# Weight sums of a seven-product matmul formed by accumulating DMAs instead of VectorE additions

## The chip, the cores and the metric

The kernel runs on one core of a Trainium2 chip. Its metric is the device time of one execution in microseconds, the median of several runs. The profiler records one execution on that core. Engines in the profile: PE (TensorE matmul) and PEld (its weight loads), DVE (VectorE), ACT (ScalarE), POOL (GpSimd), SP (SyncE, which here only issues DMAs).

## The reference

One layer of a hybrid decoder over 256 prompt tokens and 8 decoding sequences of one token, 264 columns in all. A half-step SwiGLU, a mixing block (mLSTM heads beside a short gated convolution), a second half-step SwiGLU, a last RMSNorm. What the change touches is the first half of both SwiGLUs:

```python
D_MODEL, D_FF = 2048, 5504
def swiglu(x, wg, wu, wd):
    return (jax.nn.silu(x @ wg) * (x @ wu)) @ wd
...
h = h + 0.5 * swiglu(rmsnorm(h, norm_ffn1[l]), ffn1_gate[l], ffn1_up[l], ffn1_down[l])
```

## The kernel before, in words

All weights come from HBM as f32 in blocks of 128 x 128. Each is multiplied in three f16 products: ACT writes the f16 high part (`high`), DVE the f16 remainder (`low`), and PE takes high x high, high x low, low x high. A SwiGLU has 43 column blocks j of gate (g) and up (u). An ordinary block is two `product` calls, g and u, of 16 k blocks each, made in two halves of 8 k blocks: 24 matmuls a half. Before each half stands a `fetch`: SP loads 512 KB of weights that are used five halves later (`wraw`, six buffers), ACT writes `whi`, DVE writes `wlo`.

For 11 of the 43 blocks in the first SwiGLU and 12 in the second (`SEVEN`), gate and up together are made by Strassen's scheme in Winograd's form: seven products of half size instead of eight. The weight's four quarters are g and u, each with an upper and a lower half of the k blocks; the tokens are split in a left and a right half of 132, whose sums are the `forms`. `chunk_by_seven` makes the products in two chunks: chunk 0 (72 matmuls of 132 columns) with three quarters as they are, from the tiles `sa0` (high) and `sa1` (low); chunk 1 (96 matmuls) with four sums of quarters, from `sb0` and `sb1`. The order of the blocks from a seven-block j on is: chunk 0 of j, the ordinary block j + 1 (four halves), chunk 1 of j, the ordinary block j + 2 (four halves), chunk 0 of the next seven-block. One such block is a period of the program.

The tiles for the chunks are prepared in small steps between the halves: after each half's matmuls and its fetch, `prepare_step` takes the next step of a table (`prepare`). There are 8 steps per seven-block, and the table says at which step of its block a function runs: POOL issues four loads of 512 KB (`load`, tile `sraw`, at steps -2 and -1), ACT and DVE cut the three quarters into `sa0` and `sa1` (`blocks`, `blocks_low`, steps 2 to 4), DVE forms the four sums in `ssum` by three additions or subtractions per half (`all_sums`), and ACT and DVE cut these into `sb0` and `sb1` (steps 5 to 8). Chunk 0 follows step 7, chunk 1 follows step 11, which is step 3 of the next block. All of a block's data is loaded in the block before, into two buffers. The first block of a layer runs its steps three earlier. The steps stop during most of the down products between the 22nd and 23rd column block.

Nothing reorders the instructions: each engine runs its queue in the order in which the code issues it and waits on semaphores. `Norm.form` builds the sums of token halves on POOL; `by_seven` adds the seven products up on DVE; `activated` multiplies silu(g) by u and cuts the result for the down product. A check of sums decides at the end whether a second, slower pass is run.

Of the kernel before, what the change touches and what calls it, by code (L numbers as in the profile page):

```python
# [8 lines left out]
F32 = mybir.dt.float32  # L9
# [3 lines left out]
ALU = mybir.AluOpType  # L13
# [38 lines left out]
TH = T // 2  # L52
# [93 lines left out]
def step(ctx: ExitStack, tc: tile.TileContext, a: dict, shared, bad=None):  # L146
    nc = tc.nc
# [70 lines left out]
    def high(dst, src, scale=1.0):  # L218

        if half_size or not isinstance(scale, float):  # L220
            nc.scalar.activation(dst, src, AF.Copy, scale=scale)  # L221
        else:
            nc.scalar.copy(dst, src)
# [49 lines left out]
    def at(delta, fn, *args):  # L273
        agenda.setdefault(int(seq[0]) + delta, []).append((fn, args))
# [43 lines left out]
    def prepare(pool, layer):  # L318

        gu = a[f"w{layer}gu"]
        ks = [slice(0, 4), slice(4, 8)]
        raws = [None, None]
        steps.clear()
        step_no[0] = None

        def load(j, c):
            raws[c] = raw = pool.tile([128, 4, 4, 128], F32, tag="raw", name="sraw", bufs=2)
            for g in range(2):  # L330
                blocks = gu[j, g].rearrange("p (s k) m -> p s k m", s=2)
                queue.dma_start(raw[:, 2 * g : 2 * g + 2], blocks[:, :, ks[c], :])  # L332

        def blocks(j, c):
            if c == 0:
                formed[j, 0] = [
                    pool.tile([128, 3, 8, 128], PART, tag=f"sa{i}", name=f"sa{i}")
                    for i in range(2)
                ]
            high(formed[j, 0][0][:, :, ks[c]], raws[c][:, 0:3], sw)  # L340

        def blocks_low(j, c):
            hi, lo = formed[j, 0]
            low(lo[:, :, ks[c]], raws[c][:, 0:3], hi[:, :, ks[c]], sw)

        sums = [None]

        def all_sums(j, c):
            raw = raws[c]
            if c == 0:  # L350
                formed[j, 1] = [
                    pool.tile([128, 4, 8, 128], PART, tag=f"sb{i}", name=f"sb{i}")
                    for i in range(2)
                ]
            sums[0] = s = pool.tile([128, 4, 4, 128], F32, tag="ssum", name="ssum")
            nc.vector.tensor_tensor(s[:, 2], raw[:, 2], raw[:, 3], op=ALU.add)
            nc.vector.tensor_tensor(s[:, 3], s[:, 2], raw[:, 1], op=ALU.subtract)
            nc.vector.tensor_tensor(  # L358
                s[:, 0:2], raw[:, 0:4:2],
                s[:, 3].unsqueeze(1).to_broadcast([128, 2, 4, 128]), op=ALU.subtract,  # L360
            )
            high(formed[j, 1][0][:, :, ks[c]], s, sw)

        def sums_low(j, c):
            hi, lo = formed[j, 1]
            low(lo[:, :, ks[c]], sums[0], hi[:, :, ks[c]], sw)

        for n, j in enumerate(SEVEN[layer]):
            for s, fn, c in (
                (2, blocks, 0), (3, blocks_low, 0), (3, blocks, 1), (4, blocks_low, 1),  # L370
                (5, all_sums, 0), (6, sums_low, 0), (7, all_sums, 1), (8, sums_low, 1),
            ):
                steps.setdefault(8 * n + s - (3 if n == 0 else 0), []).append((fn, j, c))
            for c in range(2):
                s = -4 if n == 0 else 8 * n + (-2, -1)[c]
                steps.setdefault(s, []).append((load, j, c))

    def prepare_step():
        if step_no[0] is not None and step_no[0] < step_end[0]:
            for fn, j, c in steps.get(step_no[0], ()):  # L380
                fn(j, c)
            step_no[0] += 1

    def chunk_by_seven(j, c, x, forms, banks):
# [242 lines left out]
    class Norm:  # L627
# [26 lines left out]
        def form(self, k):  # L654


            b = tmp.tile([128, 7, TH], F32, tag="y7", name="form_b", bufs=1)
            t = tmp.tile([128, 4, TH], F32, tag="form_t", name="form_t", bufs=2)
            for i, kb in enumerate((k + 8, k)):
                nc.scalar.activation(  # L660
                    b[:, 2 * i : 2 * i + 2].rearrange("p s t -> p (s t)"), h[kb], AF.Copy,
                    scale=gains[:, self.col + kb : self.col + kb + 1],
                )
            side.tensor_tensor(t[:, 0:2], b[:, 1:4:2], b[:, 0:2], op=ALU.subtract)
            side.tensor_tensor(t[:, 2], b[:, 3], t[:, 0], op=ALU.subtract)
            side.tensor_tensor(t[:, 3], t[:, 2], b[:, 2], op=ALU.subtract)
            self.parts = t

        def form_split(self, k):
# [56 lines left out]
    def ffn(layer, norm, done, start=None, end=None):  # L726
        with ExitStack() as stack:
# [10 lines left out]
            first = True  # L738
            seven = {}

            def activated(j, i, zu, sg):
                nc.vector.tensor_tensor(zu, zu, sg, op=ALU.mult)
                act[j] = t = apool.tile([128, 2, T], PART, tag=f"a{i}", name=f"a{i}")
                high(t[:, 0, :], zu, sa[layer])
                rest = t[:, 1, :], zu, t[:, 0, :], sa[layer]
                if lag[0] and j < blocks[-1] - 2:
                    at(1.5, low, *rest)
                else:
                    low(*rest)

            def by_seven(j, i):


                p, q, r = (b[:, : 3 * TH].rearrange("p (n t) -> p n t", n=3) for b in seven[j])
# [24 lines left out]
                at(1, halves)  # L779
                at(2, activated, j, i, z[:, 1], sg)  # L780

            if half_size:
                spool = stack.enter_context(tc.tile_pool(name=f"seven_{norm.tag}", bufs=1))
# [896 lines left out]
```

## Time and profile before

| | |
|---|---|
| median of 3 runs | 1814.26 us (1813.57 to 1816.54) |
| span of the profiled execution, first to last instruction | 1812.0 us |
| PE busy | 1796.6 us |
| DVE, ACT, POOL busy | 1391.5, 958.0, 250.2 us |
| HBM read | 366.72 MB |
| POOL's loads of sraw | 92 of 512 KB |

The profiled execution's own device time is not among the figures; its span stands in for it, 2.3 us below the median. A row of the profile reads: line, engine, operation, tile written <- tiles read, shape, count | busy time in all, mean ns of one | idle time of the engine just before, and what ended it. PE's matmuls overlap, so that a row's mean is longer than the distance from one to the next.

### The profile page before, as it was taken

To read this page: it belongs to the slowest core of one execution; us is meant where nothing else is said; L and a number is where in the kernel's file an instruction comes from. 1 tells how busy PE (TensorE), PEld (TensorE's weight loads), DVE (VectorE), ACT (ScalarE), POOL (GpSimd) and SP (SyncE) were. 2 spreads that over 40 slices of the span, in tenths; PEclk is the share of its full clock that TensorE was granted. 3 is DMA by queue.
4 is the path that set the end of the run, shared out by engine and by line. 5 is a ranking of instruction groups with operands and counts; after the bars stand their busy time and mean duration, and the time that the engine had idled before them with its cause. 6 is when DMAs were issued, how large, how long until landed. Compare 5 with 4: busy or idle time off the path is not lost.

```text
span 1812.0 us, 42493 instructions
## 1 busy us (share of the span) xinstructions
PE 1796.6 (99%) x17920; PEld 1590.5 (88%) x17920; DVE 1391.5 (77%) x2132; ACT 958.0 (53%) x1329; POOL 250.2 (14%) x339
## 2 busy tenths in 40 slices
PE   9999999999999999999999999999999999999997
PEld 7889988899998888888888888889988889999886
DVE  7888985579997667788888766789986459998554
ACT  7664554445554444667566645655554435554442
POOL 0310000000100222222121022410000001010131
PEclk9999999999999999999999999999999999999999
DMA  9765666645654565988887655756567646564663
GB/s 300 251 219 170 218 225 212 202 157 191 217 189 151 187 190 193 307 279 273 282 282 241 221 179 185 253 191 221 190 187 257 199 147 213 193 209 155 190 193 97
DMA packets 118503, 381.34 MB, mean 210 GB/s; under 512 B 14972, under 2 KB 24796, under 8 KB 118304
## 3 DMA queue, kind: packets, MB, share of 16 engines
q1 hardware_dynamic: 95856, 302.29, 51.1%
q0 software_dynamic: 21504, 75.81, 12.4%
q8 instruction: 142, 2.33, 0.5%
q10 hardware_dynamic: 944, 0.45, 0.1%
q14 instruction: 57, 0.47, 0.1%
HBM read 366.72 MB, written 11.78 MB: 209 GB/s over the span
## 4 chain that ended last, share of the span: by engine, by line
PE 98%; DVE 1%; DMA 0%; ACT 0%; issue 0%; SPq 0%; DVEq 0%; ACTq 0%
PE ps L288 28%; PE ps L290 28%; PE ps L289 28%; PE ps L410 12%; PE ps L506 1%; PE ps L624 0%; PE ps L1349 0%; PE ps L1292 0%; PE ps L1247 0%; DMA wraw<-in_w1gu 0%; DVE sq L698 0%; DVE h L918 0%; PE ps L1270 0%; PE ps L1333 0%; PE ps L1271 0%; ACT whi L221 0%
## 5 line engine op out<-in xcount | busy, mean ns | idle before, releaser
L229 DVE SCALAR_TENSOR_TENSOR wlo<-wraw,whi 128x1024 f16<-128x1024 f32 (+2 forms) x600 | 695.2, 1181 | 97.3 <-ACT whi L221 96.9
L221 ACT ACTIVATE whi<-wraw 128x1024 f16<-128x1024 f32 (+2 forms) x600 | 585.0, 1001 | 202.3 <-PE ps L289 166.8
L290 PE MATMUL ps<-x,wlo 128*128 128x264 f16 x1952 | 539.4, 276 | 0.0
L288 PE MATMUL ps<-x,whi 128*128 128x264 f16 x1952 | 539.4, 276 | 0.0
L289 PE MATMUL ps<-x,whi 128*128 128x264 f16 x1952 | 539.4, 276 | 0.0
L289 PEld LDWEIGHTS <-whi 128*128 128x128 f16 x4522 | 442.2, 98 | 66.4
L288 PEld LDWEIGHTS <-whi 128*128 128x128 f16 x4522 | 442.5, 98 | 65.3 <-issue 0.6
L290 PEld LDWEIGHTS <-wlo 128*128 128x128 f16 x4522 | 442.3, 98 | 65.2
L288 PE MATMUL ps<-a,whi 128*128 128x264 f16 (+2 forms) x1418 | 383.3, 273 | 0.0
L289 PE MATMUL ps<-a,whi 128*128 128x264 f16 (+2 forms) x1418 | 383.3, 273 | 0.0
L290 PE MATMUL ps<-a,wlo 128*128 128x264 f16 (+2 forms) x1418 | 383.2, 273 | 0.0
L288 PE MATMUL ps<-xm,whi 128*128 128x264 f16 x896 | 247.6, 276 | 0.0
L289 PE MATMUL ps<-xm,whi 128*128 128x264 f16 x896 | 247.6, 276 | 0.0
L290 PE MATMUL ps<-xm,wlo 128*128 128x264 f16 x896 | 247.6, 276 | 0.0
L221 ACT ACTIVATE sb<-ssum 128x2048 f16<-128x2048 f32 x46 | 87.9, 1910 | 177.3 <-DVE ssum L358 177.3
L410 PEld LDWEIGHTS <-sb 128*128 128x128 f16 x2208 | 128.8, 98 | 0.7
L860 DVE SCALAR_TENSOR_TENSOR h<-ps,h 128x264 f32<-128x264 f32 x62 | 26.8, 432 | 130.5 <-PE ps L290 130.5
L229 DVE SCALAR_TENSOR_TENSOR sb<-ssum,sb 128x2048 f16<-128x2048 f32 x46 | 105.3, 2289 | 6.0 <-ACT sb L221 3.6
L410 PE MATMUL ps<-f,sb 128*128 128x132 f16 x1656 | 99.0, 221 | 0.0
L410 PEld LDWEIGHTS <-sa 128*128 128x128 f16 x1656 | 97.1, 98 | 0.7
L332 POOL DMA_DIRECT2D sraw<-in_w2gu x48 | 34.6, 722 | 420.3 <-issue 382.0
L332 POOL DMA_DIRECT2D sraw<-in_w1gu x44 | 31.7, 723 | 392.5 <-issue 359.3
(256 smaller groups left out, 1665.9 us busy)
## 6 DMA issues: line engine op xcount, KB each, us to landing
wraw<-in_w2gu SPq DMA_DIRECT2D x124, 512.0 KB, 4.6
wraw<-in_w1gu SPq DMA_DIRECT2D x120, 512.0 KB, 4.9
wraw<-in_win SPq DMA_DIRECT2D x112, 512.0 KB, 5.6
wraw<-in_w1d SPq DMA_DIRECT2D x80, 448.0 KB, 4.1
wraw<-in_w2d SPq DMA_DIRECT2D x80, 448.0 KB, 3.8
sraw<-in_w2gu POOLq DMA_DIRECT2D x48, 512.0 KB, 5.3
sraw<-in_w1gu POOLq DMA_DIRECT2D x44, 512.0 KB, 5.3
wraw<-in_wout SPq DMA_DIRECT2D x32, 512.0 KB, 4.8
```

Source lines behind the costliest of these rows:

```text
L221: nc.scalar.activation(dst, src, AF.Copy, scale=scale)
L229: nc.vector.scalar_tensor_tensor(dst, src, scale, hi, op0=ALU.mult, op1=ALU.subtract)
L288: nc.tensor.matmul(ps, wh, xk[:, 0, :], start=first, stop=False)
L289: nc.tensor.matmul(ps, wh, xk[:, 1, :], start=False, stop=False)
L290: nc.tensor.matmul(ps, wl, xk[:, 0, :], start=False, stop=last)
L332: queue.dma_start(raw[:, 2 * g : 2 * g + 2], blocks[:, :, ks[c], :])
L410: nc.tensor.matmul(out, w[:, f, k, :], b(k)[:, part, :], start=(k + term == 0), stop=(k == 7 and term == 2),)
L506: nc.tensor.matmul(ps[j0 + j], w[:, nk * j + k, :], x[k0 + k][:, part, :], start=(k0 + k + n == 0), stop=(k0 + k == KB - 1 and n == 2),)
L860: nc.vector.scalar_tensor_tensor(h[db], ps, 0.5 / (sw * sa[layer]), h[db], op0=ALU.mult, op1=ALU.add)
```

## The change

The signs of the scheme are turned so that the four sums of weight quarters are all plain sums: lower g + lower u; upper u + lower u; that plus lower g; that plus upper g. `sraw` now holds three quarters of a block (lower and upper as loaded by `upper` and `lower`), from which `sa` is cut. Then POOL issues DMAs with `accum_op=add` (`adds`), which add another quarter from HBM to what lies in the tile: one into two slots at once, two more into one slot. After each of them the slots concerned are cut into `sb` (`cut` for the high part on ACT, `cut_rest` for the remainder on DVE). DVE's three additions and `ssum` are gone. Since `sraw` is overwritten, an add must wait for the cuts before it, and a cut for the add before it. The turned signs cost one subtraction more per form on POOL and a negative scale in `activated`.

```diff
-        def load(j, c):
...
-            sums[0] = s = pool.tile([128, 4, 4, 128], F32, tag="ssum", name="ssum")
-            nc.vector.tensor_tensor(s[:, 2], raw[:, 2], raw[:, 3], op=ALU.add)
-            nc.vector.tensor_tensor(s[:, 3], s[:, 2], raw[:, 1], op=ALU.subtract)
-            nc.vector.tensor_tensor(
-                s[:, 0:2], raw[:, 0:4:2],
-                s[:, 3].unsqueeze(1).to_broadcast([128, 2, 4, 128]), op=ALU.subtract,
-            )
-            high(formed[j, 1][0][:, :, ks[c]], s, sw)
...
+        def upper(j):
+            raws[j] = raw = pool.tile([128, 3, 8, 128], F32, tag="raw", name="sraw", bufs=2)
+            queue.dma_start(raw[:, 2], gu[j, 1][:, 0:8, :])
+            queue.dma_start(raw[:, 1], gu[j, 0][:, 8:16, :])
+
+        def lower(j):
+            queue.dma_start(raws[j][:, 0], gu[j, 0][:, 0:8, :])
+
+        def adds(j, slots, g, s):
+            dst, src = raws[j][:, slots], gu[j, g][:, 8 * s : 8 * s + 8, :]
+            n = slots.stop - slots.start
+            if n > 1:
+                src = src.unsqueeze(1).to_broadcast([128, n, 8, 128])
+            queue.dma_start(dst, src, accum_op=ALU.add)
...
+        def cut(j, c, slots, of):
+            hi, lo = tiles(j, c)
+            high(hi[:, slots], raws[j][:, of], sw)
+
+        def cut_rest(j, c, slots, of):
+            hi, lo = tiles(j, c)
+            low(lo[:, slots], raws[j][:, of], hi[:, slots], sw)
+
+        one, two, three_ = slice(0, 1), slice(1, 3), slice(2, 3)
         for n, j in enumerate(SEVEN[layer]):
-            for s, fn, c in (
-                (2, blocks, 0), (3, blocks_low, 0), (3, blocks, 1), (4, blocks_low, 1),
-                (5, all_sums, 0), (6, sums_low, 0), (7, all_sums, 1), (8, sums_low, 1),
+            for s, fn, *what in (
+                (2, cut, 0, two, two), (3, cut_rest, 0, two, two), (3, adds, two, 1, 1),
+                (3, cut, 0, one, one), (4, cut_rest, 0, one, one),
+                (6, cut, 1, two, two), (7, cut_rest, 1, two, two), (7, adds, three_, 0, 1),
+                (9, cut, 1, slice(3, 4), three_), (9, cut_rest, 1, slice(3, 4), three_),
+                (9, adds, three_, 0, 0),
+                (11, cut, 1, one, three_), (11, cut_rest, 1, one, three_),
             ):
...
+            side.tensor_tensor(b[:, 4], b[:, 1], b[:, 0], op=ALU.subtract)
+            side.tensor_tensor(t[:, 2], b[:, 4], b[:, 3], op=ALU.subtract)
+            side.tensor_tensor(t[:, 3], t[:, 2], b[:, 2], op=ALU.add)
...
-                high(t[:, 0, :], zu, sa[layer])
-                rest = t[:, 1, :], zu, t[:, 0, :], sa[layer]
+                high(t[:, 0, :], zu, sign * sa[layer])
+                rest = t[:, 1, :], zu, t[:, 0, :], sign * sa[layer]
```

How this moves instructions is shown for the second seven-block of the first layer (j = 13) and its neighbours. The numbers behind the names tell buffers apart; the brackets name the semaphores that an instruction waits for (DMASW: one of POOL's DMAs).

POOL's queue before, over one block: the four loads of the next block, and the first of the one after.

```order
L332 DMA sraw_2237<-in_w1gu 128x2x512 [waits DMASW5_49,DMASW6_49,DVE_49,Activation_49]
L332 DMA sraw_2237<-in_w1gu 128x2x512
L332 DMA sraw_2275<-in_w1gu 128x2x512 [waits DMASW0_49,DMASW7_49,DVE_49,Activation_49]
L332 DMA sraw_2275<-in_w1gu 128x2x512
L332 DMA sraw_2717<-in_w1gu 128x2x512 [waits DMASW1_49,DMASW2_49,DVE_49,Activation_49]
```

And after: `sraw_1765` is the block's own tile, `sraw_2234` the next block's. L329, L330 and L333 are loads, L340 the adds.

```order
L340 DMA sraw_1765<-in_w1gu 128x2x1024 [waits DMASW7_49,DMASW0_49,DVE_49]
L329 DMA sraw_2234<-in_w1gu 128x1024 [waits DMASW6_49,DMASW3_49]
L330 DMA sraw_2234<-in_w1gu 128x1024
L340 DMA sraw_1765<-in_w1gu 128x1024 [waits DMASW2_49,DVE_49]
L333 DMA sraw_2234<-in_w1gu 128x1024
L340 DMA sraw_1765<-in_w1gu 128x1024 [waits DMASW5_49,DVE_49]
L340 DMA sraw_2234<-in_w1gu 128x2x1024 [waits DMASW3_49,DMASW4_49,DVE_49,Activation_49]
```

Three adds of the block now stand between the loads for the next one, each waiting for DVE (the remainder cut before it) and for a DMA.

ACT before, from step 6 to the cuts of step 11 (`sb0_2190` is the block's, `sa0_2459` the next block's; `a` and `tb` belong to ordinary blocks or to by_seven):

```order
L221 ACTIVATE whi_2232<-wraw_2230 128x1024 [waits DMAHW6_49,PE_49]
L221 ACTIVATE whi_2266<-wraw_2264 128x1024 [waits DMAHW7_49,PE_49]
L221 ACTIVATE sb0_2190<-ssum_2270 128x4x512 [waits DVE_49]
L221 ACTIVATE a12_2281<-tc_2278 128x264 [waits DVE_49]
L221 ACTIVATE whi_2388<-wraw_2386 128x1024 [waits DMAHW0_49,PE_49,Activation_49]
L221 ACTIVATE whi_2419<-wraw_2417 128x1024 [waits DMAHW1_49,PE_49,Activation_49]
L808 ACTIVATE tb_2426<-ta_2423 128x264 [waits DVE_49,Activation_49]
L221 ACTIVATE whi_2455<-wraw_2453 128x1024 [waits DMAHW2_49,PE_49,Activation_49]
L221 ACTIVATE sa0_2459<-sraw_2237 128x3x512 [waits DMASW2_49,DMASW1_49]
L221 ACTIVATE whi_2488<-wraw_2486 128x1024 [waits DMAHW3_49,PE_49,Activation_49]
L221 ACTIVATE sa0_2459<-sraw_2275 128x3x512 [waits DMASW4_49,DMASW3_49]
```

And after, the same stretch:

```order
L221 ACTIVATE whi_2227<-wraw_2225 128x1024 [waits DMAHW6_49,PE_49]
L221 ACTIVATE sb0_2231<-sraw_1765 128x2048 [waits DMASW2_49]
L221 ACTIVATE whi_2263<-wraw_2261 128x1024 [waits DMAHW7_49,PE_49]
L221 ACTIVATE a12_2273<-tc_2270 128x264 [waits DVE_49]
L221 ACTIVATE whi_2380<-wraw_2378 128x1024 [waits DMAHW0_49,PE_49,Activation_49]
L221 ACTIVATE whi_2410<-wraw_2408 128x1024 [waits DMAHW1_49,PE_49,Activation_49]
L221 ACTIVATE sb0_2231<-sraw_1765 128x1024 [waits DMASW5_49]
L806 ACTIVATE tb_2420<-ta_2417 128x264 [waits DVE_49,Activation_49]
L221 ACTIVATE whi_2449<-wraw_2447 128x1024 [waits DMAHW2_49,PE_49,Activation_49]
L221 ACTIVATE sa0_2453<-sraw_2234 128x2048 [waits DMASW4_49,DMASW3_49]
L221 ACTIVATE whi_2482<-wraw_2480 128x1024 [waits DMAHW3_49,PE_49,Activation_49]
L221 ACTIVATE sb0_2231<-sraw_1765 128x1024 [waits DMASW7_49]
```

The cuts of `sb0` no longer wait for DVE but for POOL's DMAs, and the last of them, formerly three steps before chunk 1, stands behind the last whi of step 11.

PE at the border from step 11 to chunk 1, after:

```order
L290 MATMUL ps_2422<-x115_484,wlo_2228 128x264
L405 LDWEIGHTS sb0_2231 [waits Activation_49]
L405 MATMUL ps_2277<-x10_189,sb0_2231 128x132
L405 LDWEIGHTS sb0_2231
L405 MATMUL ps_2277<-x10_189,sb0_2231 128x132
L405 LDWEIGHTS sb1_2232 [waits DVE_49]
L405 MATMUL ps_2277<-x10_189,sb1_2232 128x132
```

The first matmul of chunk 1 reads the slot that is cut last, and waits there for ACT, then for DVE; before, the same rows had no wait.

More of the change, by code (lines that the diff above doesn't have):

```diff
@@ L322, in prepare @@
         gu = a[f"w{layer}gu"]
-        ks = [slice(0, 4), slice(4, 8)]
-        raws = [None, None]
+        raws, parts = {}, {}
         steps.clear()
         step_no[0] = None
-        def load(j, c):
[L329 to L337, printed above, removed]
+        def upper(j):
+            raws[j] = raw = pool.tile([128, 3, 8, 128], F32, tag="raw", name="sraw", bufs=2)
+            queue.dma_start(raw[:, 2], gu[j, 1][:, 0:8, :])
+            queue.dma_start(raw[:, 1], gu[j, 0][:, 8:16, :])
@@ new lines, in lower, with tiles @@
+        def lower(j):
[6 more added lines that the diff above has]
+            queue.dma_start(dst, src, accum_op=ALU.add)
+        def tiles(j, c):
+            if (j, c) not in formed:
+                formed[j, c] = [
+                    pool.tile([128, 3 + c, 8, 128], PART, tag=f"s{'ab'[c]}{i}", name=f"s{'ab'[c]}{i}")
@@ L338, in blocks @@
                     for i in range(2)
                 ]
[L340 to L354, printed above, removed]
-            sums[0] = s = pool.tile([128, 4, 4, 128], F32, tag="ssum", name="ssum")
-            nc.vector.tensor_tensor(s[:, 2], raw[:, 2], raw[:, 3], op=ALU.add)
-            nc.vector.tensor_tensor(s[:, 3], s[:, 2], raw[:, 1], op=ALU.subtract)
-            nc.vector.tensor_tensor(
-                s[:, 0:2], raw[:, 0:4:2],
-                s[:, 3].unsqueeze(1).to_broadcast([128, 2, 4, 128]), op=ALU.subtract,
-            )
-            high(formed[j, 1][0][:, :, ks[c]], s, sw)
@@ L364, in sums_low @@
-        def sums_low(j, c):
-            hi, lo = formed[j, 1]
-            low(lo[:, :, ks[c]], sums[0], hi[:, :, ks[c]], sw)
-        for n, j in enumerate(SEVEN[layer]):
-            for s, fn, c in (
-                (2, blocks, 0), (3, blocks_low, 0), (3, blocks, 1), (4, blocks_low, 1),
-                (5, all_sums, 0), (6, sums_low, 0), (7, all_sums, 1), (8, sums_low, 1),
-            ):
[L373 to L376, printed above, removed]
+            return formed[j, c]
@@ new lines, in cut @@
+        def cut(j, c, slots, of):
[5 more added lines that the diff above has]
+        one, two, three_ = slice(0, 1), slice(1, 3), slice(2, 3)
+        for n, j in enumerate(SEVEN[layer]):
+            for s, fn, *what in (
[5 more added lines that the diff above has]
+                (11, cut, 1, one, three_), (11, cut_rest, 1, one, three_),
+            ):
+                steps.setdefault(8 * n + s - (3 if n == 0 else 0), []).append((fn, j, *what))
+            for fn, s in ((upper, -2), (lower, -1)):
+                s = -4 if n == 0 else 8 * n + s
+                steps.setdefault(s, []).append((fn, j))
@@ L378, in prepare_step @@
     def prepare_step():
         if step_no[0] is not None and step_no[0] < step_end[0]:
-            for fn, j, c in steps.get(step_no[0], ()):
-                fn(j, c)
+            for fn, *what in steps.get(step_no[0], ()):
+                fn(*what)
             step_no[0] += 1
@@ L663, in form @@
                 )
-            side.tensor_tensor(t[:, 0:2], b[:, 1:4:2], b[:, 0:2], op=ALU.subtract)
-            side.tensor_tensor(t[:, 2], b[:, 3], t[:, 0], op=ALU.subtract)
-            side.tensor_tensor(t[:, 3], t[:, 2], b[:, 2], op=ALU.subtract)
+            side.tensor_tensor(
+                t[:, 0:2], b[:, 0:4:3], b[:, 1:2].to_broadcast([128, 2, TH]), op=ALU.subtract
+            )
+            side.tensor_tensor(b[:, 4], b[:, 1], b[:, 0], op=ALU.subtract)
+            side.tensor_tensor(t[:, 2], b[:, 4], b[:, 3], op=ALU.subtract)
+            side.tensor_tensor(t[:, 3], t[:, 2], b[:, 2], op=ALU.add)
             self.parts = t
@@ L739, in ffn, with activated @@
             seven = {}
-            def activated(j, i, zu, sg):
+            def activated(j, i, zu, sg, sign=1.0):
                 nc.vector.tensor_tensor(zu, zu, sg, op=ALU.mult)
                 act[j] = t = apool.tile([128, 2, T], PART, tag=f"a{i}", name=f"a{i}")
-                high(t[:, 0, :], zu, sa[layer])
-                rest = t[:, 1, :], zu, t[:, 0, :], sa[layer]
+                high(t[:, 0, :], zu, sign * sa[layer])
+                rest = t[:, 1, :], zu, t[:, 0, :], sign * sa[layer]
                 if lag[0] and j < blocks[-1] - 2:
@@ L779, in by_seven @@
                 at(1, halves)
-                at(2, activated, j, i, z[:, 1], sg)
+                at(2, activated, j, i, z[:, 1], sg, -1.0)
             if half_size:
```

## Prediction

> **What bounds the kernel now.** I read the page's engine totals first, then the chain, then what PE waited for. The columns are busy time and its share of the span; in the chain, shares of the span.
>
> ```profile
> span 1812.0 us, 42493 instructions
> PE 1796.6 (99%) x17920; PEld 1590.5 (88%) x17920; DVE 1391.5 (77%) x2132; ACT 958.0 (53%) x1329; POOL 250.2 (14%) x339
> PE 98%; DVE 1%; DMA 0%; ACT 0%; issue 0%; SPq 0%; DVEq 0%; ACTq 0%
> ...
> PE ps L975 <- DVE ok L969: 2.3, 1, 2.3
> PE ps L506 <- ACT whi L221: 1.8, 2, 1.3
> PE ps L624 <- DVE sq L700: 1.2, 1, 1.2
> ```
>
> PE is the chain, and its three longest waits, all at the two ends of the program, make 5.3 us. No wait on sa, sb or a form is among them. DVE work that goes away can therefore give back nothing that shows; the question is only whether PE starts to wait. So I went to one block made by seven (layer 1, j = 13): its row in a view by stretches (PE busy, ..., clock, DMA share, GB/s), its chunks in the chain, and PE's rows at their borders.
>
> ```profile
> 147.00:178.26 31.26, 31.26 (x362) 28.44 (x361) 28.56 (x39) 16.56 (x20) 2.88 (x4) 1.00 0.61 202
> ...
> 116.83 4.14 PE ps L410 x72
> 148.09 4.14 PE ps L410 x72
> 163.03 5.52 PE ps L410 x96
> ...
> 147.92 0.57 PE L410 MATMUL ps<-x,sa 128*128 128x132 f16 x7
> 154.65 0.28 PE L290 MATMUL ps<-x,wlo 128*128 128x264 f16 x1
> 154.76 0.28 PE L288 MATMUL ps<-x,whi 128*128 128x264 f16 x1
> 162.86 0.85 PE L410 MATMUL ps<-x,sb 128*128 128x132 f16 x12
> ```
>
> A block takes 31.26 us, all of it PE, at clock 1.00, with the DMA engines busy 61%. There are 11 + 12 = 23 such blocks. The chunk on sa (4.14 us) is issued from 147.92, the chunk on sb from 162.86, and a half product of 24 matmuls takes (162.86 - 147.92 - 4.14) / 4 = 2.70 us. I count the block's steps as the table does: step 7 is the last half before the sa chunk, step 11 the last before the sb chunk. 154.76 is the start of step 9.
>
> **What is removed.** Three DVE adds per half block, and the cuts of their sums:
>
> ```profile
> L358 DVE TENSOR_TENSOR ssum<-sraw,ssum 128x1024 f32<-128x1024 f32 x46 | 56.3, 1225 | 1.6
> L357 DVE TENSOR_TENSOR ssum<-ssum,sraw 128x512 f32<-128x512 f32 x46 | 31.8, 692 | 1.6
> L356 DVE TENSOR_TENSOR ssum<-sraw 128x512 f32<-128x512 f32 x46 | 31.5, 686 | 0.0
> L229 DVE SCALAR_TENSOR_TENSOR sb<-ssum,sb 128x2048 f16<-128x2048 f32 x46 | 105.3, 2289 | 6.0 <-ACT sb L221 3.6
> L221 ACT ACTIVATE sb<-ssum 128x2048 f16<-128x2048 f32 x46 | 87.9, 1910 | 177.3 <-DVE ssum L358 177.3
> L229 DVE SCALAR_TENSOR_TENSOR wlo<-wraw,whi 128x1024 f16<-128x1024 f32 x420 | 509.5, 1229 | 51.9 <-ACT whi L221 51.7
> L221 ACT ACTIVATE whi<-wraw 128x1024 f16<-128x1024 f32 x420 | 425.9, 1044 | 100.5 <-PE ps L289 89.5 <-PE ps L1271 2.6 <-DVE wlo L229 1.9
> ```
>
> 56.3 + 31.8 + 31.5 = 119.6 us of DVE go, 5.2 us per block, all beside PE: worth 0. The seven tiles are cut either way, in five pieces now instead of four (two of 128x2048 and three of 128x1024): on ACT 2 x 1.91 + 3 x 1.04 = 6.9 us per block, on DVE 2 x 2.29 + 3 x 1.23 = 8.3 us. ACT, busy 16.56 of 31.26, and DVE, 28.56 less 5.2, cover that. The negated scale and the turned signs change constants in the same instructions: 0.
>
> **What is added on POOL.** One subtraction more per form, 16 in all. POOL's rows around the last form of layer 1 and its loads:
>
> ```profile
> 103.16 0.96 POOL L666 TENSOR_TENSOR form_t<-form_t,form_b 128x132 f32<-128x132 f32 x1
> 147.11 1.44 POOL L332 DMA_DIRECT2D sraw<-in_w1gu  x2 [28.70 <-issue]
> ```
>
> At 0.96 us each that is 15 us of an engine that is 14% busy; the last form ends at 104.1, the first chunk that reads forms starts at 116.83, so 12.7 us cover it, also with the first accumulating transfer queued ahead of that form. Worth 0. A block issues six DMAs instead of four, at 0.72 us each: 4.3 us of 31.26, no bound either.
>
> **What becomes a chain.** Before, everything needed for sb lay in SBUF when DVE turned to it. Now it comes through three transfers in a row, each held back by the cut of the tile that it changes: cut two slots, add (two slots), cut two, add (one slot), cut, add (one slot), cut; and the sb chunk reads the slot cut last first. I call the landing times of the last two adds D. Where the chain starts is read from DVE and ACT before:
>
> ```profile
> 143.89 0.69 DVE L356 TENSOR_TENSOR ssum<-sraw 128x512 f32<-128x512 f32 x1
> 146.48 0.43 DVE L805 TENSOR_TENSOR ta<-ps,rstd 128x264 f32<-128x264 f32 x1
> 146.90 0.42 DVE L742 TENSOR_TENSOR y<-y,tb 128x264 f32<-128x264 f32 x1
> 148.41 0.41 ACT L808 ACTIVATE tb<-ta 128x264 f32<-128x264 f32 x1
> 148.72 0.41 ACT L221 ACTIVATE a<-y 128x264 f16<-128x264 f32 x1
> 149.04 1.99 ACT L221 ACTIVATE whi<-wraw 128x1024 f16<-128x1024 f32 x2
> ```
>
> Without the adds ta starts at 143.9 instead of 146.5. ACT then goes tb at 144.3, a 0.31 later, whi another 0.32 later (the spacings of the rows), and after 0.95 us of whi the cut of step 6 at 145.9. It ends at 145.9 + 1.91 = 147.8, the rest on DVE at 147.8 + 2.29 = 150.1: issue of the second add. It lands at 150.1 + D; cut 1.04, rest 1.23: the third add goes out at 152.4 + D, lands at 152.4 + 2D, and its cut ends at 153.4 + 2D. PE wants that tile at 162.86, so it is late by 2D - 9.4; and the rest, 1.23 us later, is wanted two matmuls (0.1 us) after the tile: another 1.1. PE waits **2D - 8.3 us per block**.
>
> There is a floor that doesn't depend on the second add. The cut of step 9 stands on ACT behind that step's whi, whose buffer PE frees with the last matmul of step 8 (154.65 + 0.28 = 154.9; that ACT waits for PE there is the 89.5 us in whi's row). It starts no earlier than 154.9 + 0.95 = 155.9, the third add goes out at 155.9 + 1.04 + 1.23 = 158.2, and the last cut ends at 159.2 + D. PE waits at least **D - 2.55 us per block**; this rules from D = 5.8 down.
>
> Behind the waiting cut stand, on ACT, the next block's single-slot cut of sa, a of the neighbouring product and m of the sb chunk; on DVE the next block's rests; on POOL its first add. None of them has a reader that PE reaches before the sb chunk, and the weights of the four halves after it are cut before the wait. So the wait itself is all that PE sees.
>
> **The price D.** No transfer of this trace accumulates. The nearest rows, landing times from issue (sraw over the whole run; sraw around this block; rb and SP's weights, as listed by issue; the POOL queue's packets, MB and share of the engines):
>
> ```profile
> DMA to landing us min/median/max: 4.3/5.3/12.3
> DMA to landing us min/median/max: 4.7/5.1/6.7
> rb<-dr POOLq DMA_DIRECT2D x16, 512.0 KB, 8.3
> ...
> wraw<-in_w1gu SPq DMA_DIRECT2D x120, 512.0 KB, 4.9
> q0 software_dynamic: 21504, 75.81, 12.4%
> ```
>
> An add of 512 KB must bring the old 512 KB as well as the new: as many bytes read as a pair of plain loads. The pair's second goes out 0.72 us after the first and lands at most 6.7 later here: D = 7.4. The lower end is a plain load: 4.3 at least, 5.1 as a rule. Above stand rb with 8.3 and the longest sraw, 12.3. I take 7.4, the row with the same bytes to read. Then PE waits 2 x 7.4 - 8.3 = 6.5 us per block, 23 x 6.5 = 150 us, and the span is 1812.0 + 150 = 1962. The median of the runs, 1814.26, lies 2.3 above the profiled span, which I add: **1964 us**. I keep 23 alike: the first block of a layer starts three steps earlier, the one at j = 22 has two of its adds done during the down products, and the second of a layer follows a block that started early; these go both ways.
>
> The first add (two slots) is no bound at this price. By q0's row a pass of 512 KB takes 0.124 x 1812 x 0.524 / 75.81 = 1.55 us of all engines; two passes more than a one-slot add make 7.4 + 3.1 = 10.5. It goes out when both rests that follow the stalled chunk's start are done, 1.1 + 2.29 = 3.4 us after that start, and is wanted at step 6: the sb chunk's 5.52 and its wait of 1.1, four halves of 2.70, less the 2.0 from 145.9 to 147.92, are 15.4 after it. It has 12.0 us.
>
> [...]
>
> **Rivals.**
> 1. The adds land like plain loads, D = 4.3 to 5.8. Then the floor rules: at 5.1, 2.55 x 23 = 59 us, 1873 us (1854 at 4.3). For it: engines idle 39% of a block; the adds go out alone. Against: the bytes.
> 2. Dearer adds, D over 9. At 10 the wait is 11.7 us a block, 2083 us; at the longest row, 12.3, 16.3 and 2189, where the transfers themselves come near to the pace. 0.61 x 31.26 = 19.1 us of engine time now move the twelve transfers of 512 KB of a block, 6.3 MB; the new block loads 5.8 MB plainly and writes 2.1 MB by adds, at twice the time per byte 30 us, at four times 43 us, more than a block has. For it: one wait adds to the next, and SP's weights share the engines. Against: SP's loads land in 4.9 us beside POOL's today, rb's in 8.3.
> 3. Not slower: the whole chain is hidden, and PE keeps its 1796.6 us. The place is the last add, the point D <= 2.55 from the floor. The time would be 1814, no less, since there is no PE wait to recover. Against: no sraw load, none of them an add, landed in under 4.3.
>
> A wrong sum would send the program into its second pass and roughly double the time; the signs work out on paper, and I give that nothing of its own.
>
> **How the numbers follow.** Forecast (D from 5.8 to 9, 1890 to 2037): 0.55. Rival 1: 0.20. Rival 2: 0.20. Rival 3: 0.05, of which 0.02 for a gain from something I don't see. The range leaves about one in ten on each side: low 1866, between D = 4.3 and 5.1 of rival 1; high 2090, D = 10. A measurement of this kernel can tell about 0.2% (3.6 us) from no change: faster 0.02, same 0.03, slower 0.95.
>
> **What would show it.** In the new trace PE's waits have one large entry, on sb from the cuts and their rests, some 23 times each and nowhere else; the sb chunks lie 31.3 + 6.5 us apart; the sa chunk still follows without a gap; clock 1.00; the three ssum lines are gone and DVE is busy about 120 us less. A landing time of about 7.4 for the one-slot adds shows D, about 10 or 11 for the first. What would make it wrong: D far from 7.4 either way, each us of it being 46 us of time; ACT reaching the cut of step 6 later than 145.9, each us 23; or waits of PE on whi, which would mean that ACT, held by its waits for the adds, no longer keeps the plain weights ahead.

## The result, and the profile after

The changed kernel takes 1963.85 us in the median (1958.47 to 1971.83), the kernel before 1813.91 us beside it: a ratio of 1.083, interval 1.080 to 1.086. The profiled execution took 1971.83 us, with a span of 1970.1, so 158.1 us more than the profiled span before; it was the longest of the four executions. The prediction said 1964. As will be seen, two of its errors cancelled.

From the page of the kernel after: span, PE's and DVE's busy time, POOL's DMA queue (packets, MB, share of the engines' time), the chain by engine. Then what PE waited for (us in all, times, longest), and the landing times of all accumulating transfers.

```profile
span 1970.1 us, 42493 instructions
PE 1847.4 (94%) x17920; PEld 1630.0 (83%) x17920; DVE 1282.2 (65%) x2017; ACT 968.2 (49%) x1352; POOL 300.4 (15%) x401
q0 software_dynamic: 31072, 111.99, 23.9%
PE 51%; DMA 17%; issue 16%; DVE 10%; ACT 5%; POOL 0%; DVEq 0%; ACTq 0%; POOLq 0%; SPq 0%
```

```profile
PE ps L405 <- ACT sb L221: 87.8, 22, 8.0
PE ps L405 <- DVE sb L229: 20.9, 23, 1.0
```

```profile
DMA to landing us min/median/max: 5.4/6.7/10.7
```

PE was 98% of the chain and is now 51%; DMA, ACT and DVE, which did not count, share the rest. Two waits have appeared, both at the head of the sb chunk and nowhere else: 87.8 + 20.9 = 108.7 us. That leaves 158.1 - 108.7 = 49.4 us without a wait. They are in PE's own busy time: 1847.4 against 1796.6, for the same 17920 matmuls. Where they come from shows in a view by stretches (PE busy with its count, ..., granted clock, DMA share, GB/s): one whole block first, then the stretch of the wait and the two that follow it.

```profile
446.31:483.31 37.00, 33.20 (x361) 29.95 (x361) 23.76 (x34) 16.98 (x20) 4.66 (x6) 0.95 0.79 214
...
478.50:483.31 4.81, 1.01 (x10) 0.51 (x7) 1.28 (x2) 2.36 (x3) 0.00 (x0) 1.00 0.79 266
483.31:487.00 3.69, 3.69 (x38) 3.69 (x39) 3.25 (x5) 0.42 (x1) 0.99 (x2) 0.57 0.00 0
487.00:490.35 3.35, 3.35 (x59) 3.35 (x57) 0.18 (x1) 0.00 (x0) 1.38 (x3) 0.96 0.63 95
```

A block took 31.26 us before and takes 37.00 here. Of the 5.74 us more, 37.00 - 33.20 = 3.80 are PE standing still (one of the shorter waits; the mean is 108.7 / 23 = 4.7), and 33.20 - 31.26 = 1.94 are PE working for longer on the same instructions. The last two rows say why: right after the wait the granted clock is 0.57 for about 3.7 us, then it is back at 0.96. That is (1 - 0.57) x 3.69 + (1 - 0.96) x 3.35 = 1.6 + 0.1 = 1.7 us of full clock less. In the same 3.69 us the DMA engines moved nothing at all (share 0.00), so that traffic can't be what holds PE there.

The chain of this block, in order of time (start, us, what; L405 is the sb chunk), shows the wait's origin:

```profile
461.80 1.81 ACT sb L221
...
463.63 2.30 DVE sb L229
465.93 0.29 issue
466.22 5.38 DMA sraw<-in_w1gu
...
471.65 2.95 issue
...
474.61 6.31 DMA sraw<-in_w1gu
...
480.94 1.06 ACT sb L221
...
482.03 1.24 DVE sb L229
...
483.31 7.22 PE ps L405 x94
```

What ACT and DVE did in the 2.95 us after the second add had landed:

```profile
471.05 1.06 ACT L221 ACTIVATE whi<-wraw 128x1024 f16<-128x1024 f32 x1 [2.91 <-PE ps L289]
472.01 1.04 ACT L221 ACTIVATE sb<-sraw 128x1024 f16<-128x1024 f32 x1
...
473.08 1.23 DVE L229 SCALAR_TENSOR_TENSOR sb<-sraw,sb 128x1024 f16<-128x1024 f32 x1 [3.16 <-ACT sb L221]
```

These are the links that the prediction strung together: the cut of two slots, its rest, the second add (5.38 us to land), the third (6.31), the last cut and rest. The 2.95 us between the two adds are mostly work: the second add lands at 466.22 + 5.38 = 471.60, its cut starts 0.4 us later, behind the whi of step 9 on ACT, and the cut and its rest take 2.3 us. The chunk that follows takes 7.22 us for 94 matmuls; before, all 96 took 5.52.

### The profile page after: what moved, and what is told of

The parts are those of the page before. It is cut to its first block, busy times and chain, and to the rows that moved or that the text cites. A ratio compares the mean times of both kernels' runs of the same rounds, so it can differ in the third digit from the quotient of the medians.

```text
span 1970.1 us, 42493 instructions
## 1 busy us (share of the span) xinstructions
PE 1847.4 (94%) x17920; PEld 1630.0 (83%) x17920; DVE 1282.2 (65%) x2017; ACT 968.2 (49%) x1352; POOL 300.4 (15%) x401
## 3 DMA queue, kind: packets, MB, share of 16 engines
q0 software_dynamic: 31072, 111.99, 23.9%
## 4 chain that ended last, share of the span: by engine, by line
PE 51%; DMA 17%; issue 16%; DVE 10%; ACT 5%; POOL 0%; DVEq 0%; ACTq 0%; POOLq 0%; SPq 0%
PE ps L288 13%; PE ps L290 13%; PE ps L289 13%; DMA sraw<-in_w2gu 9%; DMA sraw<-in_w1gu 8%; PE ps L405 8%; DVE sb L229 4%; ACT sb L221 3%; DVE wlo L229 2%; DVE sa L229 1%; ACT whi L221 1%; PE ps L501 1%; DMA wraw<-in_w1gu 1%; DVE ta L803 0%; PE ps L619 0%
## 5 line engine op out<-in xcount | busy, mean ns | idle before, releaser
L405 PEld LDWEIGHTS <-sb 128*128 128x128 f16 x2208 | 167.0, 116 | 120.2 <-ACT sb L221 94.1
L229 DVE SCALAR_TENSOR_TENSOR sb<-sraw,sb 128x1024 f16<-128x1024 f32 (+1 forms) x69 | 109.1, 1581 | 225.9 <-ACT sb L221 225.9
L405 PE MATMUL ps<-x,sb 128*128 128x132 f16 x552 | 62.9, 296 | 108.8 <-ACT sb L221 87.8
L221 ACT ACTIVATE sb<-sraw 128x1024 f16<-128x1024 f32 (+1 forms) x69 | 92.1, 1335 | 95.0 <-DMA sraw<-in_w2gu 51.9
L405 PE MATMUL ps<-f,sb 128*128 128x132 f16 x1656 | 117.8, 241 | 0.0
L340 POOL DMA_DIRECT2D sraw<-in_w2gu x36 | 35.2, 976 | 515.2 <-DVE sb L229 373.0
L340 POOL DMA_DIRECT2D sraw<-in_w1gu x33 | 32.6, 988 | 478.4 <-DVE sb L229 354.0
```

What stands on the lines that cost most here:

```text
L229: nc.vector.scalar_tensor_tensor(dst, src, scale, hi, op0=ALU.mult, op1=ALU.subtract)
L340: queue.dma_start(dst, src, accum_op=ALU.add)
L405: nc.tensor.matmul(out, w[:, f, k, :], b(k)[:, part, :], start=(k + term == 0), stop=(k == 7 and term == 2),)
```

## The experiments

For each run the table splits the profiled span above the 1812.0 us of before into PE's waits on sb (or, in the pauses, on the copies) and the rest. In the second row 67.3 us of added matmuls (26 x 0.1125 x 23; 24 of them take 2.70 us) are taken off as well. Below, the regular blocks are the 17 of the 23 other than the first two of each SwiGLU and the one in each that the down products split.

| kernel | median us | ratio to before | span | waits | rest |
|---|---|---|---|---|---|
| after | 1963.85 | 1.083 (1.080 to 1.086) | 1970.1 | 108.7 | 49.4 |
| PE kept busy while it waits | 1940.50 | 1.069 (1.066 to 1.071) | 1941.4 | 39.8 | 22.3 |
| plain loads for the adds | 1870.41 | 1.031 (1.029 to 1.033) | 1870.6 | 41.8 | 16.8 |
| late slot last | 1895.48 | 1.047 (1.044 to 1.051) | 1891.4 | 55.0 | 24.4 |
| last add on DVE | 1844.86 | 1.017 (1.015 to 1.018) | 1845.7 | 24.8 | 8.9 |
| chain begun earlier | 1946.09 | 1.072 (1.070 to 1.074) | 1946.3 | 92.4 | 41.9 |
| begun earlier, late slot last | 1826.30 | 1.007 (1.005 to 1.010) | 1821.3 | 6.9 | 2.4 |
| late slot last, last add on DVE | 1825.27 | 1.005 (1.004 to 1.007) | 1823.7 | 6.2 | 5.5 |
| all three | 1827.86 | 1.007 (1.006 to 1.009) | 1824.3 | 9.5 | 2.8 |
| before, with 3 copies as a pause | 1989.65 | 1.096 (1.094 to 1.098) | 1991.6 | 127.0 | 52.6 |
| before, with 6 copies | 2023.01 | 1.114 (1.112 to 1.116) | 2022.1 | 154.2 | 55.9 |
| before, with 9 copies | 2043.01 | 1.125 (1.124 to 1.127) | 2041.8 | 181.5 | 48.3 |

### The slot cut last is read last

```diff
-        for f, (ps, col, b) in enumerate(work):
+        places = (1, 2, 3, 0) if c == 1 else (0, 1, 2)
+        for place, f in enumerate(places):
+            ps, col, b = work[f]
```

> Only the order of the products in the sb chunk changes: the slot that is cut last is read last instead of first. Theory (the loss is the wait of PE for the last tile of a chain of transfers, 4.7 to 5.7 us per block, and a lower granted clock just after so long a wait): the other 72 matmuls of the chunk, 4.1 us, now run ahead of that tile, so 0.6 to 1.6 us of wait per block remain, too short to cost the clock: 1812 + 23 x 1.1 + 2 = about 1840, 1825 to 1855. Rival (the transfers, or ACT's and DVE's queues behind them, take 37 us per block whatever PE reads first): the blocks stay 37 us apart and the time is 1930 or more.

1895.48 us lies between the two expectations. 68 of the 23 x 4.1 = 94 us of cover came back: over two stretches of six blocks the sb chunks are 34.6 and 35.6 us apart on average, where the changed kernel has 37.9 and 38.2. The chain of one such block shows what holds them there:

```profile
437.63 1.92 ACT sb L221
...
439.57 2.30 DVE sb L229
...
442.16 7.39 DMA sraw<-in_w1gu
...
452.20 5.83 DMA sraw<-in_w1gu
...
458.06 1.06 ACT sb L221
...
460.29 2.29 DVE sa L229
...
463.12 9.24 DMA sraw<-in_w1gu
...
472.44 1.92 ACT sb L221
```

No PE is in it. It runs from the cut before the second add (437.63) over the second and third add, the last cut, and the rest of sa's cut (460.29), which stands behind it on DVE, to the first add of the next block (463.12), which lands 9.24 us later and releases the next cut at 472.44. That is a loop of 34.8 us, closed by the order of the queues alone: the table lets the first add of a block begin only behind the last cut of the block before. The theory had the wait right and missed that the chains of two blocks are linked.

### PE is kept busy while it waits

```diff
+        if c == 1:
+            for _ in range(26):
+                nc.tensor.matmul(q[:, :T], ones16, x[0][:, 0, :], start=True, stop=True)
```

> Adds 26 matmuls of 264 columns (about 2.9 us) right before every sb chunk, where PE waits anyway; their results are overwritten. The chain of transfers is untouched, so that the last tile comes when it did. Theory (two losses per block: about 5.2 us of waiting and about 1.7 us in which the sb chunk runs at a lower granted clock because PE stood still): with about 2.4 us of standing still left the clock stays at 0.99 or above and the chunk goes at its 5.5 us: 1964 - 23 x 1.7 = about 1925, 1915 to 1940. Rival (the lower clock is not caused by standing still, or the chunk is slow for other reasons, such as its tiles arriving late): 1955 to 1970. If the added matmuls came on top of the wait, 1964 + 23 x 2.9 = 2030.

1940.50: 23.4 us less than the changed kernel, with 2.9 us more of work per block. The added matmuls went into the wait (39.8 + 67.3 = 107.1, against 108.7), and the rest fell from 49.4 to 22.3. So lost clock is a second loss, beside the wait; the rival is out, though the time lies just above the expected range. That it fell by 27 and not to nothing agrees with the pauses that were left: after 7 of the 22 the matmuls of the chunk still start slow, against 21 of 23 in the changed kernel.

### Plain loads in place of the adds

```diff
-            queue.dma_start(dst, src, accum_op=ALU.add)
+            queue.dma_start(dst, src)
...
-                at(2, activated, j, i, z[:, 1], sg, -1.0)
+                at(2, activated, j, i, z[:, 1], sg, -1.0 / 64)
```

> The three accumulating transfers of a block are plain loads of the same size to the same place, with the same waits around them; the sums of quarters are left out, and the cut of by_seven's result is scaled by 1/64 so that the numbers stay finite. Theory (adding makes a transfer land about 1 us later, 6.2 against about 5.1 us): the wait falls to D - 2.55 = 2.5 us per block and the clock stays up: 1812 + 23 x 2.5 + 2 = about 1872, 1855 to 1900. Rival 1 (a chain of transfers costs this whether they add or not): 1950 to 1970. Rival 2 (adding costs far more, and plain loads hide altogether): 1814 to 1830.

1870.41 against an expected 1872, and again by two errors that cancel: the waits are 41.8 us, not 2.5 x 23 = 58, and the clock did not stay up (the rest is 16.8). The queue's row, and the landing times of the three transfers of a regular block (1594.4 to 1627.6):

```profile
q0 software_dynamic: 31072, 111.99, 18.4%
...
DMA to landing us min/median/max: 4.0/4.3/6.2
```

The same view of a block of the changed kernel (446 to 483):

```profile
DMA to landing us min/median/max: 5.4/6.3/8.9
```

So adding costs 1.4 to 2.7 us of landing time in these two blocks. Over all 23 blocks a one-slot transfer took 6.5 us on average with the adding and 4.7 without, a two-slot one 9.4 and 6.5. And adding takes nearly twice the engines' time: the same 111.99 MB took 0.239 x 1970.1 = 471 us there and 0.184 x 1870.6 = 344 here, 127 us more. The adds carry 23 x 4 x 0.524 = 48.2 MB of it; at this run's 344 / 111.99 = 3.07 us per MB they took 148 us as loads, so 275 as adds, 1.9 times as much (an estimate, since it takes the plain packets to have cost the same in both runs). About 94 of the 150 us of the change hang on the adding (1963.85 - 1870.41 = 93.4); the other 57 are the price of a chain of loads with cuts between, whatever the loads do.

### The last add on DVE

The third add's summand lies in slot 0 of the same tile, so DVE can make it.

```diff
-                (9, adds, three_, 0, 0),
-                (11, cut, 1, one, three_), (11, cut_rest, 1, one, three_),
+                (9, add_here), (10, cut, 1, one, three_), (10, cut_rest, 1, one, three_),
...
+        def add_here(j):
+            r = raws[j]
+            nc.vector.tensor_tensor(r[:, 2], r[:, 2], r[:, 0], op=ALU.add)
```

> One link of the chain is undone: the third add of a block, whose summand lies in slot 0 of the same tile, is made by DVE (128x1024, about 1.23 us) instead of a transfer, and its cut goes out one step earlier (step 10). The other two adds stay transfers. Theory (PE waits for the sum of two landing times): one landing time of about 6.2 goes and 1.2 us of DVE come in, which is more than the 5.2 us of wait with the step gained: no wait on sb is left, the clock stays 1.00, and the time is 1812 to 1825, taken 1816. Rival (each accumulating transfer costs its share, by traffic or by the queues): two thirds of the 150 us stay, about 1914.

1844.86: one link of three gone, and 119 of the 150 us with it. That is far from two thirds of the loss staying, so the loss does not go by the number of adds. The edit also brings the last cut forward by a step; the two were not tried apart. And 24.8 us of waits are left where none was expected. The chain of one block, from DVE's add on:

```profile
471.47 1.22 DVE sraw L344
472.69 0.06 DVE ta L806
...
473.13 0.06 ACT tb L809
...
473.46 1.04 ACT whi L221
474.50 0.96 ACT sb L221
...
475.48 1.24 DVE sb L229
```

The sum is done at 472.69, but its cut has to let the tb and whi of step 10 go first on ACT, and tb waits for ta, which stands behind the add on DVE. These 1.7 to 1.8 us between the sum and its cut are there in all 17 regular blocks. The first add is not what holds the blocks here: in the regular ones the cut of step 6 starts 0.1 to 3.3 us after it has landed.

### The chain begun earlier, alone and with the late slot last

```diff
-                (2, cut, 0, two, two), (3, cut_rest, 0, two, two), (3, adds, two, 1, 1),
+                (0, cut, 0, two, two), (1, cut_rest, 0, two, two), (1, adds, two, 1, 1),
...
-                (6, cut, 1, two, two), (7, cut_rest, 1, two, two), (7, adds, three_, 0, 1),
-                (9, cut, 1, slice(3, 4), three_), (9, cut_rest, 1, slice(3, 4), three_),
-                (9, adds, three_, 0, 0),
-                (11, cut, 1, one, three_), (11, cut_rest, 1, one, three_),
+                (5, cut, 1, two, two), (6, cut_rest, 1, two, two), (6, adds, three_, 0, 1),
+                (8, cut, 1, slice(3, 4), three_), (8, cut_rest, 1, slice(3, 4), three_),
+                (8, adds, three_, 0, 0),
+                (10, cut, 1, one, three_), (10, cut_rest, 1, one, three_),
...
-            for fn, s in ((upper, -2), (lower, -1)):
+            for fn, s in ((upper, -4), (lower, -3)):
```

The second kernel leaves the last cut at step 11 and reads that slot last.

> All three adds stay transfers and PE still reads the slot cut last first. The chain begins two to three halves earlier: the two slots of sa are cut at step 0 and their rests at step 1, where the first add goes out (before: 2 and 3); the cut before the second add moves from step 6 to 5, the third add from 9 to 8, the last cut from 11 to 10; the plain loads go out at steps -4 and -3 instead of -2 and -1. Theory (a chain of three transfers and their cuts takes about 34.5 us when its first add waits behind the last cut of the block before, and a block of PE only 31.3; begun earlier, the chains of two blocks overlap): the wait mostly goes, 1815 to 1840, taken 1828. Rival (adds occupy the transfers' engines too long, about twice a plain load's time per byte, and this sets the pace of a block): 1900 or more.

> The earlier chain (sa cut at step 0, first add at 1, second at 6, third at 8, loads at -4 and -3, last cut at step 11) and in addition the slot cut last is read last by PE, which gives the last link 4.1 us more. Theory: both losses of the change are gone while it still has all its transfers: 1813 to 1825, taken 1818, clock 0.99 or more. Rival (traffic of the adds): no better than 1880.

Alone it missed: 1946.09, not 1828. Its rows from one block: the sb chunk after its wait, the issue of the second add, a stretch of its flight, and the landing times of the adds issued in it (437 to 474: the block's second and third, and the next block's first).

```profile
437.04 2.45 PE L405 MATMUL ps<-x,sb 128*128 128x132 f16 x22 [0.97 <-DVE sb L229]
```

```profile
454.80 0.88 POOL L340 DMA_DIRECT2D sraw<-in_w1gu  x1 [15.85 <-DVE sb L229]
```

```profile
457.00:460.00 3.00, 3.00 (x47) 2.88 (x45) 1.50 (x2) 0.84 (x1) 0.00 (x0) 1.00 0.91 201
```

```profile
DMA to landing us min/median/max: 6.5/8.5/10.4
```

The second add went out 454.80 - 437.04 = 17.8 us after the sb chunk had resumed, where the changed kernel had 466.22 - 446.31 = 19.9. So 2.1 us were won at its issue, but it took 8.5 us to land instead of 5.4, and the third add 6.5. Over all 23 blocks the second add took 7.7 us on average, 6.4 in the changed kernel. From 457 to 460 the DMA engines were 91% busy. What made it slow was not tried apart; that SP's loads of plain weights, which run beside the adds, are the cause is a guess. D is no constant, and on what it depends stays open.

With the late slot last in addition it is 1826.30, a little above the expected 1813 to 1825, with the lowest waits but one:

```profile
PE ps L407 <- ACT sb L221: 3.6, 2, 3.3
PE ps L407 <- DVE sb L229: 3.3, 5, 1.0
```

It moves the same bytes by the same adds (q0 111.99 MB), and 138 of the 150 us are gone. So nearly all of the cost is not the traffic of the adds but the time at which the last link ends. Neither edit does it alone: one leaves the loop, the other a last link that ends mostly 2 to 4 us late.

### Late slot and DVE add; all three

> The third add on DVE with its cut at step 10, and in addition the slot cut last is read last. Theory (with two transfers the chain is about 32 us long, of which some 1 us is PE's own wait that delays the next block; the 4.1 us of the other 72 matmuls hide it): 1812 to 1822, taken 1816. Rival (what is left of the loss in the run with the third add on DVE, 31 us, comes from the transfers of the other two adds or from ACT's queue): it stays at 1835 to 1845.

> The two milder cures and the shorter chain together: the third add on DVE, the first add at step 1 (second at 6, third sum at 8, last cut at 10, loads at -4 and -3), and the slot cut last read last. Theory (PE is the bound again as soon as every tile of sb is there when its matmuls stand next): no wait on sb is left anywhere, the first blocks of the layers included, and the time is that of the kernel before, 1812 to 1819, taken 1815; no less than 1812, since PE's own work is unchanged. Rival (two adding transfers of a block still cost something through the weights' loads, which they slow down: about 11 us in each of the two best runs so far): 1822 to 1828.

1825.27 and 1827.86: both lie above their ranges, which stood for no loss, and all three edits together bring nothing over two. The runs of these kernels spread over 4 to 10 us. Of the 11 to 13 us that are left, 6 to 10 are waits on sb. With two edits the chains of two blocks are still linked: the last rest of five blocks in a row ends 2.2, 2.9, 4.0, 4.2 and 4.8 us after the start of its sb chunk, until the cover of some 4.1 us is used up and PE waits, and in each of the five the cut of step 6 starts 0.1 us after the first add has landed. With all three, 3.5 us are one wait in the second block of the first SwiGLU, and 5.2 fall in four blocks of the second whose second add took 8.4 to 10.0 us to land. The 1822 to 1828 of the last rival hold the measured time, but not in the way that it gave: PE's waits on whi make 0.7 us. Why those adds land late, and the 3 to 6 us beside the waits, I have not settled. None of the cures brings the change below the kernel before: PE's own work is what it was, and was the bound.

### A pause of PE without any adds

The kernel before, sums on DVE, with ACT copies between two PSUM banks ahead of the sb chunk (3, 6 or 9 of them); `last[0]` is the finished half's bank.

```diff
+            src = last[0]
+            for i in range(9):
+                nc.scalar.copy(q[:, :T], src)
+                src = q[:, :T]
```

> The kernel before, with its sums on DVE, and in it a pause of PE right before every sb chunk: ACT copies the finished half from one PSUM bank to another, 3 times in a row (about 0.3 us each after the first), into the bank that the chunk's first matmul writes. Nothing of the transfers is changed. The pause should be 1.2 to 2 us. Theory (a pause of PE costs itself, and 1.7 us more where the granted clock falls after it; in the runs so far blocks with pauses under 1.6 us kept the clock): 23 x 1.5 = 35 us more and few dips, 1835 to 1870, clock 0.99 or more. Rival (the clock falls for another reason, the traffic of the adds): no dip here whatever the pause.

> The same with 6 copies in a row: a pause of about 2.2 to 3 us. [...] Rival (the traffic of the adds lowers the clock): no dips, 1874, and the same clock as in the kernel before.

> The same with 9 copies in a row: a pause of about 3.2 to 4 us. Theory (a pause above 3.4 us always costs the clock): 23 x (3.6 + 1.7) = 122 us more, about 1936, 1915 to 1955; the 22 matmuls that follow the first two take up to 2.6 us instead of 1.44. Rival (standing still costs nothing beyond itself): 1814 + 23 x 3.6 = 1897, clock 0.99 or more.

The pauses came out far longer than meant, 6.1, 7.3 and 8.4 us in a regular block, because the copies stand on ACT behind all that is left of step 11: whi, two cuts of sa, and an a that waits for DVE. So the short pauses were not tried. But the question, whether standing still costs clock without any add near, is answered. Waits, the row of one block's chunk, and a view of the stretch that follows the wait, with 3 copies:

```profile
PE ps L415 <- ACT ps L409: 127.0, 23, 6.7
...
452.12 2.80 PE L415 MATMUL ps<-x,sb 128*128 128x132 f16 x24 [6.08 <-ACT ps L409]
...
452.12:455.50 3.38, 3.38 (x32) 3.38 (x32) 0.00 (x0) 0.00 (x0) 0.00 (x0) 0.50 0.05 18
```

24 matmuls take 2.80 us, and the granted clock is 0.50. The same group in the kernel before:

```profile
162.86 1.54 PE L410 MATMUL ps<-x,sb 128*128 128x132 f16 x24
```

The rest beside the waits is 52.6, 55.9 and 48.3 us, 2.1 to 2.4 a block, and doesn't grow with the pause, as a fixed price per restart would have it. With 6 and with 9 copies, too, every one of the 23 chunks starts slow. The changed kernel's 49.4 is of the same size.

## Why the prediction came out right, point by point

**Where the loss is: right.** The wait is at the head of the sb chunk, 22 and 23 times, on the last cut and its rest; sa, forms and whi have none that counts. Nothing came back for the DVE work that went away (109.3 us, against about 120 said).

**The working of the wait: right.** In the block shown the second add landed after 5.38 us and the third after 6.31. With these in place of 2D, the chain gives 5.38 + 6.31 - 8.3 = 3.39 us, and the floor, D - 2.55, gives 6.31 - 2.55 = 3.76; PE stood still for 3.80. So the floor rules in this block, by 0.4 us, the time for which the landed tile lay behind whi. It does so in 3 of the 17 regular blocks; in the other 14 the cut of step 9 starts within 0.1 us of the second landing, and the sum of the two landing times rules, as the prediction took it. With each block's own landing times, the larger of the two formulas meets the wait within 0.1 us in 16 of the 17.

**The size of D: wrong.** The step that failed is "I take 7.4, the row with the same bytes to read": no run shows an add reading the old bytes. What the runs show is the landing: the 46 one-slot adds took 6.5 us on average (5.4 to 8.9): 2 x 0.9 us a block too much, 41 us of waiting over 23 blocks. By the estimate above an add does cost the engines 1.9 times the time of a load, but that is a small part of the landing: 512 KB are 3.07 x 0.524 = 1.6 us of all engines as a load and 3.0 as an add, 1.4 more, and the one-slot adds took 6.5 - 4.7 = 1.8 more to land than the same transfers without adding. The prediction had 7.4 - 5.1 = 2.3 more, for a second load. The first, two-slot add landed in 9.4 us on average (10.5 said, 12.0 allowed).

**"I keep 23 alike": right in the sum only.** The waits run from 0.8 us, in the first block of the first SwiGLU, to 8.8 (8.0 and 0.9 in two parts), in the second block of the second. But these do go both ways: the mean landing times of second and third add, 6.37 and 6.67, give 13.04 - 8.3 = 4.74 us a block, 109 in all, and the rows have 108.7.

**"Clock 1.00": wrong, a term that is missing.** 49.4 us of the loss is PE running slower after its waits: 21 of the 23 chunks start slow (some 0.3 us a block of it is put down to two restarts, an estimate from a matmul's 0.28 us against the 0.11 from one to the next). The prediction listed the clock among its signs and never asked what a wait does to it. So 150 us of waiting were forecast, and 108.7 of waiting and 49.4 of clock came. That the sum was met is luck: a D that was too long stood in for the clock. A reader should take the terms.

**The rivals.** Rival 1, adds like plain loads with D up to 5.8, was wrong: 4 of the 46 one-slot adds landed within 5.8 us. Its 1873 is near what plain loads do take (1870), but with less waiting and some lost clock. Rival 2's feared crowding did not come: DMA share 0.79 in a block of 37.00 us is 29 us of engine time, the 30 that it gave for twice the time per byte, but the pace is set by the landing times in a row. Rival 3 fell with D above 2.55, though 1826 was within reach by a different order.

## What to carry to other kernels

Before handing an addition to a DMA, count the links: an engine's 1.2 us between two cuts became 5 to 9 us of landing here, and a chain of them has to fit into one period together with everything that the queues' order ties to its ends. Read the last-made tile last, and let the next block's chain begin before this one's ends; alone they brought 68 and 18 us here, together 138. When a change makes PE wait, price each pause twice: its length, and, where the clock falls (here after 15 of 33 pauses of 1.8 to 3.4 us and after all 46 longer ones), the slow clock after it (here some 2 us a block: 49.4 us in 23 blocks).

## What the hardware showed that I had not expected

The clock fell after a pause less than half as long as those of the changed kernel, 4.7 us on average. Two blocks of the kernel that reads the late slot last; each pause is in two parts with two matmuls between (the bracket has the idle time).

```profile
492.84 0.29 PE L407 MATMUL ps<-x,sb 128*128 128x132 f16 x2 [1.10 <-ACT sb L221]
494.10 2.28 PE L407 MATMUL ps<-x,sb 128*128 128x132 f16 x22 [0.97 <-DVE sb L229]
...
528.67 0.29 PE L407 MATMUL ps<-x,sb 128*128 128x132 f16 x2 [1.61 <-ACT sb L221]
529.93 1.44 PE L407 MATMUL ps<-x,sb 128*128 128x132 f16 x22 [0.97 <-DVE sb L229]
```

After 2.07 us of pause the 22 matmuls took 2.28 us in one block, after 2.58 us they took 1.44 in the other. Over the changed kernel and the first seven variants of it, by the same rows: none of 61 chunks after a pause of up to 1.75 us starts slow (22 matmuls in more than 1.44 us), 15 of 33 between 1.8 and 3.4 us do, and all 46 above. In the changed kernel alone, 21 of 23 start slow, all after a pause of 3.46 us or more; the other two pauses were 0.84 and 2.60 us.

How long the clock stays down is in the trace as well. At the chunks on sb of the changed kernel it is 0.50 in 21 stretches, one for each chunk that starts slow: nine of 3.41 us, ten of 6.83 and two of 10.24. Each begins a whole number of times 3.413 us after the first. Here are stretches of 3.41 us around the two pauses, laid so that one of them is the lowered one (PE busy first, granted clock ahead of the DMA share):

```profile
491.08:494.49 3.41, 1.34 (x21) 0.99 (x19) 1.67 (x2) 2.00 (x2) 0.00 (x0) 1.00 0.71 281
494.49:497.90 3.41, 3.41 (x27) 2.86 (x25) 2.97 (x6) 0.58 (x2) 1.10 (x2) 0.50 0.02 5
...
525.21:528.62 3.41, 1.85 (x33) 1.68 (x30) 0.00 (x0) 1.06 (x2) 0.00 (x0) 1.00 0.50 198
528.62:532.04 3.42, 2.40 (x32) 2.12 (x33) 3.39 (x3) 0.95 (x1) 0.00 (x0) 1.00 0.03 8
532.04:535.45 3.41, 3.41 (x33) 2.97 (x31) 2.83 (x10) 0.58 (x2) 2.37 (x3) 1.00 0.27 25
```

The pause of 2.07 us falls into one of them, in which PE is idle for 61%, and the clock of the next is 0.50. The pause of 2.58 us is cut by them into parts idle for 46% and 30%, and the clock stays at 1.00. With the changed kernel's trace cut up the same way, from the start of a lowered stretch, 539 stretches of 3.413 us have clock 1.00. In 22 of them PE is idle for 59% or more, by its records, and the next has clock 0.50 each time, the last at the end of the program; in the other 517 it is idle for 58% or less, and the next has 1.00. That is a count in one trace; what lowers the clock is not shown by it. A stretch of 3.41 us at 0.50 in which PE works is 1.7 us of full clock less, as in the block of the changed kernel above.

Second, one accumulating transfer of 512 KB took from 5.4 to 8.9 us to land in the 23 blocks of the changed kernel alone, and up to 10.0 in the kernel with all three edits. A chain planned with one number for it missed in another order of the same transfers: begun earlier, it took 1946.09 us where 1828 was expected.
